# Moving modulation sums and mLSTM's end within the projection stage of a hybrid decoder block

## The chip, the cores and the metric

The kernel runs on one core of a Trainium2 chip. A core has five engines that run side by side and meet only at semaphores: PE (TensorE, matrix products and transposes), DVE (VectorE), ACT (ScalarE), POOL (GpSimd) and SP (SyncE, which here issues every DMA). Each engine works through its own instructions strictly in order, so an instruction that waits holds up all that stand behind it on the same engine. The metric is the device time of one execution in microseconds (us); lower is better. Numbers of lines (L1045) are those of the kernel before unless it is said otherwise.

## The reference, cut to what matters

One decoder layer with 2048 positions of width 1024, in float32:

```python
mod = silu(c) @ w_ada + b_ada          # six vectors of 1024: shift, scale, gate, twice
sh1, sc1, gt1, sh2, sc2, gt2 = split(mod, 6)
h = rms_norm(x, g_mix) * (1 + sc1) + sh1
p = h @ w_in                            # q,k,v (512 each), q_m,k_m,v_m,o_m (256), u_s,v_s (256), gates
y_attn = forgetting_attention(rms_norm(q_a), rms_norm(k_a), v_a, f_a)      # 8 heads of 64
hm = mlstm_chunkwise(q_m, k_m, v_m, i_m, f_m)                              # 4 heads of 64
hm = rms_norm(hm, g_m_out)                                                 # over each head's 64
y_mlstm = sigmoid(o_m) * hm
y_sgu = spatial_gating(gelu(u_s), gelu(v_s), g_sgu, w_s, b_s)
x = x + gt1 * (concat(y_attn, y_mlstm, y_sgu) @ w_out)
h = rms_norm(x, g_ffn) * (1 + sc2) + sh2
x = x + gt2 * conv_ffn(h, w_up, w_conv, b_conv, w_down)
```

The first shift and scale are needed ahead of everything. The other four vectors (two gates, second shift and scale: 4096 columns) are needed only after the mixer, and the kernel works them out in small portions beside the projections.

## The kernel before, in words

The kernel runs through the projections (about 60 to 720 us), the attention, the output product and the channel MLP. Only the projections concern the change.

*Blocks and steps.* The 2048 positions are taken in two halves of 1024; for each half the columns of `w_in` are taken in seven blocks, in this order: k_m with the gates, q_m with o_m, v_m, the spatial unit (u and v), k, q, v. That makes 14 blocks, counted from 0: the spatial unit is block 3 (first half) and 10 (second half), k is 4 and 11, q is 5 and 12, v is 6 and 13. A block has eight row tiles of 128 positions. A float32 product is made of three products of rounded parts (`mm3`, L53 to L56), so a tile is 8 x 3 = 24 matmuls on PE. After the tile's 12th matmul, in blocks 512 columns wide, and after its last, `products` calls `tick`: 16 steps in a wide block, 8 in a narrow one. Behind a tile's last step the block's own work on that tile is issued (`consume`): for q and k the squares L768 on ACT, their sums L770 on DVE, the inverse root on POOL (L128, called `rsqrt`); one step later the scaling `qn` L776 on DVE; three steps after that the four transposes L784 on PE, then L788 on ACT and L789 on DVE. For the spatial unit: a layer norm per tile (L705 to L722, with POOL's L712 and L128 in it), and after every fourth tile four mixes (PE's L735, DVE's L736 and L737; groups 0 and 1 in one step, 2 and 3 in the next) and two turns (L744). PE's results for these pass through a few shared banks, so a matmul into a bank waits until the last result in it has been read.

*A step* (`tick`) does three things. First it issues what `after(n, f)` has put off until this step. Then, at middle steps alone (those after the 12th matmul), it takes one step of `chores`, which holds the modulation sums. Then it takes one step of the first generator in `background`: `rows` and `mlstm`, first come, first served, each advancing to its next `yield`. Blocks 1 to 5 and 8 to 12 keep the order as it is written here; blocks 0, 6, 7 and 13 are put in order by the framework's scheduler.

*Modulation sums* (`rest_of_mod`, from L452). There are eight column groups of 512, each the sum over eight row tiles of `w_ada`: 64 sums. A sum is one DVE instruction of 128x512 (L466 for the first of a group, L468 for the others); it issues the load of the next 256 KB tile of `w_ada` on SP (L458). The seventh also loads the bias row; with the eighth, DVE adds that row (L474), and two steps later `columns_or_row` makes either four narrow matmuls (L488, for shift and scale) or one 512-wide one (L482, for the gates, with ACT's L484 and a store behind it).

*mLSTM* (`mlstm(qi)`, qi = 0 to 3, 512 positions each) works through four chunks of 128 positions and then has an end. `mlstm(0)` and `mlstm(2)` enter the queue in block 2 and 9, and run beside the spatial unit; `mlstm(1)` and `mlstm(3)` follow them and run beside k and q. The end is: DVE makes the denominator (L1029 to L1032) and divides (L1034, 128x1024); SP loads the gate `om` (L1036); ACT squares (L1038, into `hq`); DVE sums the squares (L1040) and scales (L1041); POOL raises to the power -1/2 (L1042, 128x16). Two steps later DVE multiplies, `hq = hn * ss` (L1045, 128x1024). Two steps later PE makes eight transposes of `hq` (L1052), and DVE multiplies by the norm's weight and by `om` (L1054) and SP stores.

*Beside these*, `products` splits the next block's weights into two parts: ACT's cast L595 and DVE's difference L596, and loads them (L585). In front of the first half's v block, SP also loads the first four row tiles of `x` for the second half (L404), which ACT squares (L518) and DVE scales (L523).

*At block 13* a loop ran what was left in `background` to its end before the score matmuls of the attention's first heads (L206) entered it.

Of the kernel before, what the change touches and what calls it, by code (L numbers as in the profile page):

```python
# [12 lines left out]
ALU = mybir.AluOpType  # L13
# [20 lines left out]
def trunk(  # L34
# [7 lines left out]
    V, A, G, T = nc.vector, nc.scalar, nc.gpsimd, nc.tensor  # L42
# [4 lines left out]
    def bc(ap, axis, n):  # L47
        u = ap.unsqueeze(axis)
        shape = list(u.shape)
        shape[axis] = n  # L50
        return u.broadcast_to(shape)
# [86 lines left out]
    def attention_open_right():  # L138
        pool.open("att_s", "right", ("nm", 8, 6), ("rs", 8, 6))
        pool.open("att_r", "right", ("kvA", 8192, 3), ("LA", 4096, 8), ("qA", 2048, 6))  # L140
        pp.open("att_r", "right", ("sp", 4096, 2))
# [19 lines left out]
    def load_v(h, cs):  # L161
        for c in cs:
            dma(
                kv[h][2][:, 4 * c : 4 * c + 4].bitcast(F32),
                v_d[c * TB : (c + 1) * TB, h, :].rearrange("(n p) d -> p n d", p=P),
            )
# [208 lines left out]
    def misc_ps():  # L375
        return pp.tile([P, 512], F32, name="mp", tag="mp")
# [25 lines left out]
    def load_x(tt):  # L402
        xt = pool.tile([P, D], F32, name="xt", tag="t4k")
        dma(xt, x[tt * P : (tt + 1) * P, :])  # L404
        return xt
# [43 lines left out]
    def rest_of_mod():  # L449

        seq = [(col, k) for col in (3072, 3584, 4096, 4608, 2048, 2560, 5120, 5632) for k in range(KT)]
        tiles = {}  # L452

        def load(i):
            if i < len(seq):
                col, k = seq[i]
                tiles[i] = pool.tile([P, 512], F32, name="wa", tag="t2k")
                dma(tiles[i], w_ada[k * P : k * P + P, col : col + 512])  # L458

        load(0)  # L460
        yield
        for i, (col, k) in enumerate(seq):
            st = tiles.pop(i)
            if k == 0:
                acc = pool.tile([P, 512], F32, name="modacc", tag="macc")
                V.tensor_scalar(acc, st, cs[:, 0:1], None, op0=ALU.mult)  # L466
            else:
                V.scalar_tensor_tensor(acc, st, cs[:, k : k + 1], acc, op0=ALU.mult, op1=ALU.add)  # L468
            load(i + 1)
            if k == 6:  # L470
                brow = pool.tile([1, 512], F32, name="brow", tag="t2k")
                dma(brow, b_ada[:, col : col + 512])
            if k == 7:
                V.tensor_tensor(acc[0:1, :], acc[0:1, :], brow, op=ALU.add)  # L474
                after(2, lambda acc=acc, col=col: columns_or_row(acc, col))
            yield

    def columns_or_row(acc, col):
        kind, half = col // 1024, (col % 1024) // 512
        ps = misc_ps()  # L480
        if kind in (2, 5):
            T.matmul(ps, ones, acc, start=True, stop=True)  # L482
            gr = pool.tile([1, 512], F32, name="gr", tag="t2k")
            A.copy(gr, ps[0:1, :])  # L484
            dma(gt_d[kind // 3 : kind // 3 + 1, half * 512 : half * 512 + 512], gr)
        else:
            for j in range(4):
                T.matmul(ps[:, j : j + 1], acc[:, j * P : (j + 1) * P], ones[:, 0:1], start=True, stop=True)  # L488
            sl = slice(half * 4, half * 4 + 4)
            if kind == 3:  # L490
                V.tensor_copy(sh2[:, sl], ps[:, 0:4])
            else:
                V.scalar_tensor_tensor(
                    a2[:, sl], ps[:, 0:4], 1.0, gf[:, half * 4 : half * 4 + 4], op0=ALU.add, op1=ALU.mult
                )
# [126 lines left out]
    pending = []  # L622
    chores, started = [], []
    background = []
    ticks = [0]

    def tick(middle=False):
        ticks[0] += 1
        due()
        if middle and chores and started and next(chores[0], True):  # L630
            chores.pop(0)
        if background and next(background[0], True):
            background.pop(0)
# [15 lines left out]
    def after(n, f):  # L649

        pending.append((ticks[0] + n, f))

    def due(everything=False):
        for item in pending[:]:
            if everything or item[0] <= ticks[0]:
                pending.remove(item)
                item[1]()
# [267 lines left out]
    def mlstm(qi):  # L925
# [52 lines left out]
        for n in range(4):  # L978
# [44 lines left out]
            if n < 3:  # L1023
                decay(n + 1)
                yield

        den = pool.tile([P, 4, 4], F32, name="den", tag="den")
        nd = pool.tile([P, 4, 4], F32, name="nd", tag="nd")
        V.tensor_scalar(nd, H[:, :, :, 64], -1.0, None, op0=ALU.mult)  # L1029
# [3 lines left out]
        hn = H[:, :, :, 0:64]  # L1033
# [2 lines left out]
        dma(om, om_d[:, :, t0 : t0 + 512].rearrange("j p t -> p j t"))  # L1036
        hq = pool.tile([P, 4, 4, 64], F32, name="hq", tag="t4k")
        A.activation(hq, hn, AF.Square)  # L1038
        ss = pool.tile([P, 4, 4], F32, name="mss", tag="mss")
        V.tensor_reduce(ss, hq, axis=AX.X, op=ALU.add)  # L1040
        V.tensor_scalar(ss, ss, 1.0 / 64, EPS, op0=ALU.mult, op1=ALU.add)  # L1041
        G.tensor_tensor(ss, ss, nhalf[:, 0:1].unsqueeze(2).broadcast_to([P, 4, 4]), op=ALU.pow)  # L1042
        yield
        yield
        V.tensor_tensor(hq, hn, bc(ss, 3, 64), op=ALU.mult)  # L1045
        hq2 = hq.rearrange("p n h d -> p n (h d)")
        yield
        yield
# [18 lines left out]
    nb = len(blocks)  # L1067
    steps = [(h, i) for h in range(2) for i in range(nb)]
    chores.append(rest_of_mod())
    written = ExitStack()  # L1070
    cur = Weights(blocks[0][0], G, ("q2k",) * 3 + ("qhl",) * 3 + ("wr",) * 2)
# [5 lines left out]
    for n, (half, i) in enumerate(steps):  # L1077
        if i == 0:
            make_h(half * 2, x0)
            if half == 0:  # L1080
                head_setup()
            make_h(half * 2 + 1)
        elif n == nb - 1:
            x0 = [load_x(8 + t) for t in range(4)]
        if n == len(steps) - 1:
            while background:
                if next(background[0], True):
                    background.pop(0)
            n_accs[0] = 2
            pool.close("proj_r")  # L1090
            pp.close("proj_r")
            attention_open_right()

            load_k(0)
            first_rows = [], []
            first = [scores(0, tb, load_q(0, tb, "qA"), r) for tb, r in zip((1, 0), first_rows)]
            load_v(0, (0, 1))
            background += first
        nxt[0] = Weights(blocks[steps[n + 1][1]][0]) if n + 1 < len(steps) else None
        if i == 1:  # L1100
            written.enter_context(tc.manual_schedule())
        blocks[i][1](half, cur)
        started.append(n)
        if nxt[0]:
            nxt[0].cast()
        cur = nxt[0]
        if n in (nb - 2, 2 * nb - 2):
            written.close()
        if i == 0:
            log_gates(half)  # L1110
            background += [rows(half * 2), rows(half * 2 + 1)]
        if i == 2:
            background.append(mlstm(half * 2 + 1))
        if n == nb + 2:
            small_setup()
# [630 lines left out]
```

## Time and profile before

| | us |
|---|---|
| three runs | 2606.87, 2607.7, 2610.26 |
| median | 2607.7 |
| the profiled execution | 2607.8 |
| its span | 2606.1 |
| PE idle in the span | 75.6 (2606.1 - 2530.5) |

The profiled execution's mean granted clock of PE is 0.997 of full speed. 1.7 us lie around the span. The page names an instruction by its engine and line, and an operand by the program's name. A "wait" is idle time of an engine ahead of an instruction, put down to the instruction elsewhere that released it. Matmuls overlap, so the durations of neighbouring ones add up to more than their distance in time: a matmul of 128x512 shows 0.39 us and the next begins 0.23 us later.

### The profile page before, as it was taken

How to read it: one execution, taken by the hardware profiler on the slowest of the kernel's cores; microseconds unless marked ns; L12 is line 12 of the kernel's file. 1: busy time of each engine (PE TensorE's matmuls, PEld its weight loads, DVE VectorE, ACT ScalarE, POOL GpSimd, SP SyncE). 2: the span in 40 equal slices, each digit the busy share in tenths (PEclk: the TensorE clock that was granted, in tenths of full speed). 3: DMA queues.
4: the chain of work that ended last, by engine and by line, in shares of the span. 5: the costliest groups of instructions: out<-in, count | busy, mean ns of one | idle time of the engine just before them, and what ended most of it. 6: DMA issues, size and time to landing. Idle time of an engine off the chain costs nothing.

```text
span 2606.1 us, 36311 instructions
## 1 busy us (share of the span) xinstructions
PE 2530.5 (97%) x12521; PEld 2097.9 (81%) x12537; DVE 2010.0 (77%) x3438; ACT 1272.8 (49%) x2424; POOL 402.5 (15%) x532
## 2 busy tenths in 40 slices
PE   5999999999999999999989999999999999999999
PEld 5888888888787877777868888888888888888787
DVE  7657666476388889866589888888888887997797
ACT  4333343432388878844455544454444444444443
POOL 2012310132266556520000000000000000000000
PEclk9999999999999999999999999999999999999999
DMA  7345763454664445266632222255222217658523
GB/s 247 107 120 160 209 209 88 129 152 138 180 164 123 129 126 166 58 195 224 248 89 92 79 89 82 81 201 187 90 81 81 90 65 279 210 176 290 184 93 117
DMA packets 302592, 379.58 MB, mean 146 GB/s; under 512 B 31934, under 2 KB 194588, under 8 KB 300360
## 3 DMA queue, kind: packets, MB, share of 16 engines
q1 hardware_dynamic: 302408, 377.26, 46.1%
q8 instruction: 99, 1.62, 0.3%
q14 instruction: 85, 0.70, 0.1%
HBM read 276.44 MB, written 100.74 MB: 145 GB/s over the span
## 4 chain that ended last, share of the span: by engine, by line
PE 81%; DVE 9%; DMA 4%; ACT 3%; issue 2%; POOL 1%; SPq 0%; DVEq 0%; ACTq 0%; POOLq 0%
PE ub L56 11%; PE ub L54 11%; PE ub L55 11%; PE acc L54 6%; PE acc L56 6%; PE acc L55 6%; PE db L55 4%; PE db L56 4%; PE db L54 4%; PE sp L206 3%; PE tp L259 3%; PE op L245 2%; PE op L246 2%; PE wps L55 2%; PE wps L54 2%
## 5 line engine op out<-in xcount | busy, mean ns | idle before, releaser
L54 PE MATMUL acc<-wh,hh 128*128 128x512 f32 (+2 forms) x768 | 285.5, 373 | 1.9 <-DVE vhl L762 1.2
L54 PE MATMUL ub<-T,wsph 128*128 128x512 f32 x704 | 274.2, 390 | 5.8 <-ACT wsph L1358 5.8
L56 PE MATMUL ub<-T,wspl 128*128 128x512 f32 x704 | 273.7, 389 | 1.6 <-DVE wspl L1359 1.6
L56 PE MATMUL acc<-wh,hl 128*128 128x512 f32 (+2 forms) x768 | 274.2, 360 | 0.3 <-DVE hl L566 0.3
L55 PE MATMUL acc<-wl,hh 128*128 128x512 f32 (+2 forms) x768 | 273.9, 358 | 0.2
L55 PE MATMUL ub<-T,wsph 128*128 128x512 f32 x704 | 273.9, 389 | 0.0
L55 PE MATMUL db<-wspl,wsph 128*128 128x512 f32 x616 | 240.6, 391 | 3.6 <-DVE wspl L1490 3.5
L56 PE MATMUL db<-wsph,wspl 128*128 128x512 f32 x616 | 239.6, 389 | 0.0
L54 PE MATMUL db<-wsph 128*128 128x512 f32 x616 | 238.3, 389 | 0.3 <-ACT wsph L1489 0.3
L1358 ACT CAST wsph<-S 128x512 fp32r<-128x512 f32 x176 | 109.7, 623 | 228.4 <-PE ub L55 162.8
L263 DVE TENSOR_TENSOR plo<-tp,phi 128x512 fp32r<-128x512 f32 (+1 forms) x320 | 187.0, 607 | 31.6 <-ACT phi L262 29.4
L54 PE MATMUL ub<-B,wsph 128*128 128x512 f32 x528 | 207.1, 392 | 2.8 <-ACT wsph L1358 2.8
L56 PE MATMUL ub<-B,wspl 128*128 128x512 f32 x528 | 207.2, 392 | 0.6 <-DVE wspl L1359 0.6
L55 PE MATMUL ub<-B,wsph 128*128 128x512 f32 x528 | 207.0, 392 | 0.0
L223 ACT ACTIVATE L<-L,nm 128x1024 f32<-128x1024 f32 (+2 forms) x192 | 172.6, 903 | 36.0 <-DVE nm L212 34.7
L262 ACT CAST phi<-tp 128x512 fp32r<-128x512 f32 (+1 forms) x320 | 160.0, 521 | 40.2 <-PE tp L259 38.9
L259 PE MATMUL tp<-ident,L 128*128 128x128 f32 x1088 | 177.0, 274 | 2.5 <-POOL L L228 0.6
L206 PE MATMUL sp<-kk,q 128*128 128x512 f32 (+3 forms) x640 | 169.2, 375 | 3.3 <-DVE nm L212 2.2
L1489 ACT CAST wsph<-act 128x512 fp32r<-128x512 f32 x132 | 82.3, 623 | 179.0 <-PE db L55 162.2
L228 POOL TENSOR_SCALAR L<-L,rs 128x1024 f32<-128x1024 f32 (+2 forms) x192 | 167.2, 881 | 11.0
L56 PEld LDWEIGHTS acc<-wh,hl 128*128 128x128 f32 x768 | 145.0, 190 | 22.3 <-DVE hl L566 0.8
L54 PEld LDWEIGHTS acc<-wh,hh 128*128 128x128 f32 x768 | 146.2, 191 | 20.7 <-DVE vhl L762 1.4
(333 smaller groups left out, 5942.9 us busy)
## 6 DMA issues: line engine op xcount, KB each, us to landing
w<-in_w_up_dram SPq DMA_DIRECT2D x88, 512.0 KB
wd<-in_w_down_dram SPq DMA_DIRECT2D x176, 256.0 KB
wa<-in_w_ada_dram SPq DMA_DIRECT2D x96, 256.0 KB
act_d<-yc SPq DMA_DIRECT2D x44, 512.0 KB
act<-act_d SPq DMA_DIRECT2D x44, 512.0 KB
wr<-in_w_in_dram SPq DMA_DIRECT2D x64, 256.0 KB
q<-q_d SPq DMA_DIRECT2D x128, 128.0 KB
hc_d<-hl SPq DMA_DIRECT2D x28, 512.0 KB
```

The costliest lines, as they stand in the source:

```text
L54: T.matmul(ps, lh, rh, start=start, stop=False, skip_group_check=resume)
L55: T.matmul(ps, lh, rl, start=False, stop=False, skip_group_check=resume)
L56: T.matmul(ps, ll, rh, start=False, stop=stop, skip_group_check=resume)
L206: T.matmul(sp[:, b : b + bw], q2[n][:, qs], kk[:, s0 + b : s0 + b + bw], start=n == 0, stop=n == 1 and not last)
L223: A.activation(L[c], L[c], AF.Exp, bias=nm[:, n - 1 : n], scale=-1.0, accum_out=rs[:, c : c + 1])
L228: G.tensor_scalar(t, t, rs[:, 0:1], 1.0, op0=ALU.mult, op1=ALU.mult)
L245: T.matmul(op[:, c0:], vv[:, j, :], hi[:, c0:], start=(j == 0), stop=False)
L259: T.transpose(tp[:, i * P : (i + 1) * P], rows[i][j // 8][:, (j % 8) * P : (j % 8 + 1) * P], ident)
L262: A.copy(hi[:, c0:], tp[:, c0:])
L263: V.tensor_tensor(lo[:, c0:], tp[:, c0:], hi[:, c0:].bitcast(F32), op=ALU.subtract)
L1358: A.copy(hi, src)
L1489: A.copy(hi, v)
```

## The change

Four edits, all in the order of work; what is computed is the same.

1. `tick` counts the steps of the running block. The modulation sums are taken in all 16 steps of block 5; at the middle steps of blocks 1, 4, 6, 8, 11 and 12 and in step 2 of block 12; and in none of blocks 3 and 10 (before: the middle steps of every wide block from block 1 on until the sums were done).
2. The column products follow the bias sum by one step, not two.
3. The end of `mlstm(0)` and `mlstm(2)` begins four steps later, so it moves from the spatial unit's last steps to the k block's first; since `mlstm(1)` and `mlstm(3)` queue behind them, these start later too, and their ends lie in the q block's steps 8 to 14 (before: 2 to 6). In every end one more step lies between the Square and its sum, and one more between the power and the product; the product L1045 is issued on POOL (L1053 of the changed kernel).
4. At block 13, the loop that empties `background` becomes an assertion that nothing is left, and that the sums are finished.

```diff
             if k == 7:
                 V.tensor_tensor(acc[0:1, :], acc[0:1, :], brow, op=ALU.add)
-                after(2, lambda acc=acc, col=col: columns_or_row(acc, col))
+                after(1, lambda acc=acc, col=col: columns_or_row(acc, col))
...
-    ticks = [0]
+    ticks, in_block = [0], [0, 0]
 
     def tick(middle=False):
         ticks[0] += 1
         due()
-        if middle and chores and started and next(chores[0], True):
+        block = started[-1] + 1 if started else 0
+        in_block[0] = in_block[0] + 1 if in_block[1] == block else 1
+        in_block[1] = block
+        if chores and (block == 5 or (block, in_block[0]) == (12, 2) or middle and block in (1, 4, 6, 8, 11, 12)) and next(chores[0], True):
             chores.pop(0)
...
+        if qi % 2 == 0:
+            for _ in range(4):
+                yield
         den = pool.tile([P, 4, 4], F32, name="den", tag="den")
...
         A.activation(hq, hn, AF.Square)
+        yield
         ss = pool.tile([P, 4, 4], F32, name="mss", tag="mss")
...
         G.tensor_tensor(ss, ss, nhalf[:, 0:1].unsqueeze(2).broadcast_to([P, 4, 4]), op=ALU.pow)
         yield
         yield
-        V.tensor_tensor(hq, hn, bc(ss, 3, 64), op=ALU.mult)
+        yield
+        G.tensor_tensor(hq, hn, bc(ss, 3, 64), op=ALU.mult)
...
         if n == len(steps) - 1:
-            while background:
-                if next(background[0], True):
-                    background.pop(0)
             n_accs[0] = 2
...
+            assert not background and next(chores.pop(), True)
             background += first
```

## The prediction

> **What bounds the kernel now.** I read the page's first part first, then its chain that ended last: TensorE is busy for 97% of the span, and four fifths of the chain is its matmuls. A change of vector work can only pay where PE itself stands.
>
> ```profile
> PE 2530.5 (97%) x12521; PEld 2097.9 (81%) x12537; DVE 2010.0 (77%) x3438; ACT 1272.8 (49%) x2424; POOL 402.5 (15%) x532
> PE 81%; DVE 9%; DMA 4%; ACT 3%; issue 2%; POOL 1%; SPq 0%; DVEq 0%; ACTq 0%; POOLq 0%
> ```
>
> The edits lie between 60 and 720 us. The view of waits, for PE alone in that stretch, gives what PE waited for there (total, times, longest, in us), all of it:
>
> ```profile
> PE mps L1052 <- DVE hq L1045: 6.8, 4, 2.7
> PE trp L560 <- ACT h L564: 2.1, 1, 2.1
> PE acc L54 <- DVE vhl L762: 1.2, 1, 1.2
> PE sp L206 <- DVE nm L212: 1.0, 3, 0.7
> PE trp L560 <- DVE xt L523: 1.0, 3, 0.5
> ```
>
> The first line is the wait of mLSTM's transposes for its last product, once per 512 positions. The view by windows places it (columns: stretch, length, then busy time of PE, PEld, DVE, ACT, POOL, the granted clock, DMA share, GB/s):
>
> ```profile
> 200.00:220.00 20.00, 17.31 (x84) 14.11 (x83) 17.28 (x37) 7.04 (x14) 9.97 (x7) 1.00 0.32 105
> 280.00:300.00 20.00, 19.12 (x99) 15.86 (x98) 12.47 (x27) 4.58 (x7) 6.13 (x3) 1.00 0.66 193
> 300.00:320.00 20.00, 20.00 (x96) 16.53 (x95) 12.60 (x23) 5.05 (x9) 6.55 (x4) 1.00 0.90 276
> 540.00:560.00 20.00, 17.31 (x81) 13.84 (x80) 15.55 (x36) 4.77 (x10) 9.50 (x7) 1.00 0.54 166
> 620.00:640.00 20.00, 19.50 (x99) 16.13 (x98) 10.61 (x19) 4.09 (x8) 9.29 (x5) 1.00 0.50 144
> ```
>
> Each 17.31 is one 2.69 us stand in a spatial unit's last steps (for positions 0 to 511 and 1024 to 1535); 19.12 and 19.50 are the stands beside the q block. Elsewhere PE is full (20.00), so any wait that arises anew there is paid in whole.
>
> The timeline at the first stand (start, us, engine, line, ...; idle before and its releaser in brackets) shows the chain:
>
> ```profile
> 203.89 1.22 DVE L1034 TENSOR_TENSOR H<-H,den 128x1024 f32<-128x1024 f32 x1
> 205.20 1.06 ACT L1038 ACTIVATE hq<-H 128x1024 f32<-128x1024 f32 x1 [10.40 <-DVE H L1034]
> 206.29 1.22 DVE L1040 TENSOR_REDUCE mss<-hq 128x16 f32<-128x1024 f32 x1 [1.19 <-ACT hq L1038]
> 207.80 3.27 POOL L1042 TENSOR_TENSOR mss<-mss,nhalf 128x16 f32<-128x16 f32 x1 [3.88 <-DVE mss L1041]
> 211.04 0.91 POOL L712 TENSOR_TENSOR ev<-ev 128x256 f32<-128x256 f32 x1
> 213.17 1.22 DVE L1045 TENSOR_TENSOR hq<-H,mss 128x1024 f32<-128x1024 f32 x1
> 214.53 1.06 PE L1052 MATMUL mps<-ident,hq 128*128 128x128 f32 x8 [2.69 <-DVE hq L1045]
> ```
>
> The power was done at 211.07, but the product went at 213.17: it stood on DVE behind the spatial unit's variance, which waited for POOL's L712, and behind a modulation sum.
>
> **The change, part by part** (line numbers of the kernel before).
>
> *The gain: 6.8 us, firmly.* The product goes to POOL, one more step lies before it, and two steps more between product and transposes remain. No row shows a 128x1024 product of two tiles on POOL. Its nearest row is the 128x256 product, L995, and the lower end is a 128x1024 product by one number per row, L228:
>
> ```profile
> L995 POOL TENSOR_TENSOR kw<-kn,ecol 128x256 f32<-128x256 f32 x16 | 9.8, 611 | 162.0 <-DMA kn<-km_d 162.0
> L228 POOL TENSOR_SCALAR L<-L,rs 128x1024 f32<-128x1024 f32 (+2 forms) x192 | 167.2, 881 | 11.0
> L468 DVE SCALAR_TENSOR_TENSOR modacc<-wa,cs,modacc 128x512 f32<-128x512 f32 x56 | 41.8, 746 | 7.4 <-DMA wa<-in_w_ada_dram 7.1
> L474 DVE TENSOR_TENSOR modacc<-modacc,brow 1x512 f32<-1x512 f32 x8 | 5.4, 679 | 0.2
> ```
>
> Four times 0.611 is 2.4 us, with 0.9 (L228) and 3.6 (four times the disturbed L712 of 0.91) as ends; I take 2.4, as L995 is the same operation. Two steps between emission and transposes are a row tile, 5.9 us (below), so the product is there in time in all four places, even where POOL starts it 2 us late. All four waits go: -6.8.
>
> *The q block's new wait: +4.9 us, once.* All 16 steps of block 5 now hold a sum (before: 8), so a column of eight sums ends at the block's 9th step, the step after mLSTM's end for positions 512-1023 begins; and its column product L488 stands one step after the bias sum L474 instead of two. So L488 enters PE's queue directly behind the next tile's transposes L784. What L474 is queued behind on DVE I time from the same stretch of before:
>
> ```profile
> 281.78 0.60 PE L784 MATMUL trp<-ident,qn 128*128 128x128 f32 x4
> 283.13 0.75 DVE L789 SCALAR_TENSOR_TENSOR qlo<-trp,colA,qhi 128x512 fp32r<-128x512 f32 x1 [0.52 <-ACT qhi L788]
> 283.80 0.17 DVE L1029 TENSOR_SCALAR nd<-H 128x16 f32<-128x16 f32 x1
> 284.71 1.22 DVE L1034 TENSOR_TENSOR H<-H,den 128x1024 f32<-128x1024 f32 x1
> 285.97 1.06 ACT L1038 ACTIVATE hq<-H 128x1024 f32<-128x1024 f32 x1 [2.87 <-DVE H L1034]
> 286.93 0.58 ACT L768 ACTIVATE qsq<-acc 128x512 f32<-128x512 f32 x1
> 288.63 0.60 PE L784 MATMUL trp<-ident,qn 128*128 128x128 f32 x4
> 293.10 0.69 DVE L776 TENSOR_TENSOR qn<-acc,ss 128x512 f32<-128x512 f32 x1 [3.75 <-POOL ss L128]
> 294.55 0.60 PE L784 MATMUL trp<-ident,qn 128*128 128x128 f32 x4
> 295.89 0.68 DVE L770 TENSOR_REDUCE ss<-qsq 128x8 f32<-128x512 f32 x1
> 296.92 1.64 POOL L128 TENSOR_TENSOR ss<-ss,nhalf 128x8 f32<-128x8 f32 x1 [3.86 <-DVE ss L771]
> ```
>
> Take L784 as 0. DVE's qlo starts at 1.35 (283.13 - 281.78); then the 8th step's sum, new there, at 2.0; mLSTM's L1029 at 2.7 (2.02 before, plus about 0.7); the division's end, 2.1 us later (283.80 to 285.93), at 4.8; ACT's Square L1038, 1.06 us and what lies between, to 5.9. The squares qsq of the tile just ended stand behind that Square on ACT, so their sum ss starts on DVE at about 6.5. From ss to qn is 2.7 us (295.89 to the end of POOL's 296.92 + 1.64, 298.56, plus a little): qn at 9.2. In the changed order the 9th step's sum comes behind qn (9.8), then L474 (10.5 to 11.2). PE reaches L488 at 5.92 (288.63 to 294.55, a tile without mLSTM) plus 0.4 of L784, 6.35. Wait: 11.25 - 6.35 = 4.9 us. The ends: 3.5, if the 8th step's sum goes late without holding L1029 and the rows' gaps are shorter; 6, if POOL's power takes 2.0 us instead of 1.64 and the bias row comes late. In the second half no column ends there, so it happens once.
>
> *The spatial unit's mixes: +2.3 us, in two places.* mLSTM's end for the half's first 512 positions now begins at the k block's first step. DVE gets the block's sum with L474 (0.75 + 0.68), then L1029 to L1034 (2.1), and PE's L735 for groups 2 and 3 needs the two transpose banks that DVE's L736 for groups 0 and 1 empties; those stand behind the first tile's qn, which waits for POOL. On POOL mLSTM's power (3.27 us above) now goes ahead of that tile's own. Before:
>
> ```profile
> 223.65 0.69 DVE L776 TENSOR_TENSOR qn<-acc,ss 128x512 f32<-128x512 f32 x1 [1.57 <-POOL ss L128]
> 225.19 0.42 DVE L736 TENSOR_TENSOR sy<-trp,gsgu 128x256 f32<-128x256 f32 x1 [0.45 <-PE trp L735]
> 228.18 1.02 PE L735 MATMUL trp<-sv,wT 128*128 128x256 f32 x4
> ```
>
> L736's first read ended at 225.61, 2.57 us before PE came with groups 2 and 3: that is the slack. With the stand gone PE comes 2.69 us earlier, at 225.49. The new chain: from the sum's start 1.4 (0.75 + 0.68), 2.1, Square 1.1, L1040 and its scaling 1.4, POOL's power 3.3, the tile's own 1.6, and 2.0 from qn to the end of the first L736 (223.65 to 225.61), 12.9 us together. If the sum starts as PE comes to its step, at 211.84 (214.53 - 2.69), the bank is free at 224.7: no wait. If DVE comes to it 3.5 us later, held by the spatial unit's last tile as before (L1045 alone kept it until 214.39), it is free at 228.2: 2.7. I take 1.2 of 0 to 2.7, near the middle: 2.3 for both halves.
>
> *The step into the v block: +2.4 us.* SP now issues three of the four loads of x back to back behind mLSTM's load of om, and in ACT's changed order four of the row squares L518 stand directly ahead of the last weight's cast, which its split on DVE needs:
>
> ```profile
> 329.12 0.64 ACT L518 ACTIVATE jk<-xt 128x512 f32<-128x512 f32 x1
> 330.93 0.67 DVE L596 TENSOR_TENSOR wl<-wr,wh 128x512 fp32r<-128x512 f32 x1
> ```
>
> Four at 0.64 are 2.6 us; about half is covered by what the old order waits for anyway, so some 1.2 us on the v block's first tile, which needs that weight; and the next column's L488, again one step behind its L474, some 1.2 more. Ends: 0 and 4.
>
> *At nothing.* The sums taken from the spatial units (8 of each) free DVE where it is 17.28 of 20 us busy; PE is full behind them but for the stand counted above. The sums in block 12 and the second half's later mLSTM lie where DVE is busy for 10.6 of 20 us; without that cover each sum would cost its 0.75. The drain loop that goes at the last block ran over an empty list. A sum's load is issued by the same step, so it moves too; in the spatial unit SP's queue is shorter by 8 loads, in block 5 longer by 8.
>
> Sum: -6.8 + 4.9 + 2.3 + 2.4 = +2.8 us. The profiled execution took 2607.8 us (a span of 2606.1 and 1.7 around it), 0.1 above the median of the runs shown: 2610.6, or 2610.5 on the median.
>
> **The rivals.**
>
> *Faster: no new wait forms.* DVE is idle for 7.5 of 20 us beside the q block; if the chain there is shorter than I count, or the order of engines gives L488 its step of room, only the gain stays: 2607.7 - 6.8 = 2601. Against it: the qn in the middle of the chain waits for POOL in nearly every tile,
>
> ```profile
> L776 DVE TENSOR_TENSOR qn<-acc,ss 128x512 f32<-128x512 f32 x32 | 22.1, 691 | 50.7 <-POOL ss L128 50.7
> ```
>
> and L474 now stands behind one.
>
> *A wash: only the q block's wait forms.* -6.8 + 4.9: 2606. For it: the spatial term and the v block's are both near the slack.
>
> *Slower: POOL's product holds up DVE.* L712 took 0.91 us beside DVE's split of weights where L995 took 0.61: the two get in each other's way. If a DVE instruction that falls into the product's 2.4 us stands until it is over, then in the q blocks qn and the sums behind it are late: qn ended at 293.79, 0.76 us before L784 at 294.55, so from 0.8 us on PE pays. That is 2.4 - 0.8 = 1.6 us at each of four products, about 6 with what DVE then lacks for sums: 2616. Against it: the row shows 0.3 us lost, by POOL, and not by DVE. [...]
>
> *Slower: late modulation weights.* The 56 sums of the L468 row waited 7.1 us for their loads. Issued at twice the rate beside block 5, the loads could come late again by as much in all, where DVE has no room to catch up (past 0.8 us a tile): 2610.5 + 7, 2617.
>
> **The numbers.** Forecast 0.45, only the q block's wait 0.15, no new wait 0.1, DVE held by POOL 0.2, late weights 0.1. A measurement of this kernel tells about 0.2%, 5.2 us, from no change: faster is below 2602.5, slower above 2612.9. Faster: the case without waits and a little of the wash, 0.12. Slower: the last two, and a part of the forecast whose terms run to their upper ends (6, 5.2 and 4 give +8.4): 0.34. The rest, 0.54, is the same. The low end takes in most of the case without waits, 2602; the high end the held DVE, 2616.
>
> **What would show it.** In the changed profile: no wait of L1052 for hq on PE (if one is left, the gain is wrong); PE's L488 beside the first half's q block waiting for DVE's L474 for 4 to 5 us (if below 1, the faster cases hold); the third and fourth L735 behind L736, twice; a gap before the v block's first tile. [...] The forecast is wrong if PE's idle time between 60 and 720 us falls by more than 4 us or grows by more than 9.

## The result, and the profile after

The changed kernel takes 2621.74 us (median of 5 runs, 2621.31 to 2624.18), the kernel before 2606.87 (5 runs, 2604.58 to 2610.26): a ratio of 1.0059, 95% interval 1.0046 to 1.0073. The forecast was 2610.5 in a range up to 2616. The profiled execution of the changed kernel has a span of 2619.7 us, 13.6 more than that of before. (Line numbers of the changed kernel lie a little behind those of before: L1052 is L1060 there, L1045 is L1053, L784 is L787, L735 is L738; L468 to L488 are the same.)

From the page of the changed kernel, its line of engines and the chain that ended last:

```profile
PE 2537.6 (97%) x12537; PEld 2101.7 (80%) x12537; DVE 2009.9 (77%) x3434; ACT 1272.9 (49%) x2424; POOL 405.8 (15%) x536
...
PE 77%; DVE 10%; DMA 5%; ACT 3%; issue 3%; POOL 2%; SPq 1%; DVEq 0%; ACTq 0%; POOLq 0%
```

PE is busy 7.1 us longer, though the work is the same: most of that, as the rows below show, is work at a lower clock. The mean granted clock was 0.992 to 0.994 in all five executions; the kernel before, in its executions beside the experiments, had 0.994 to 0.998. The chain went less through PE and more through DVE, DMA and POOL. PE's waits between 60 and 720 us (total, times, longest, in us):

```profile
PE mp L488 <- DVE modacc L474: 6.8, 2, 4.7
PE mp L482 <- DVE modacc L474: 5.2, 1, 5.2
...
PE mps L1006 <- DVE sc L992: 1.5, 2, 0.8
...
PE trp L738 <- DVE sy L739: 1.0, 4, 0.4
...
PE acc L55 <- DVE wl L596: 0.4, 1, 0.4
```

The 6.8 us in front of mLSTM's transposes are gone altogether. In their place stand 12.0 us in front of column products: 4.7 beside the first half's q block, 2.05 on the way into the v block, 5.2 at the end of block 12. The stretches of 20 us (stretch, length, then busy time of PE, PEld, DVE, ACT, POOL, granted clock, DMA share, GB/s) show a second loss behind each of them:

```profile
200.00:220.00 20.00, 20.00 (x98) 16.66 (x97) 13.41 (x31) 7.10 (x14) 9.11 (x7) 1.00 0.49 157
300.00:320.00 20.00, 15.27 (x66) 12.61 (x65) 12.65 (x25) 5.32 (x9) 8.37 (x4) 0.83 0.73 231
340.00:360.00 20.00, 17.95 (x79) 14.59 (x78) 12.89 (x29) 3.87 (x10) 1.53 (x3) 0.91 0.69 204
660.00:680.00 20.00, 14.80 (x56) 11.02 (x55) 13.26 (x23) 4.72 (x9) 4.63 (x3) 0.83 0.78 213
```

PE is full now in the spatial unit's last steps (20.00 in place of 17.31), with DVE at 13.41 in place of 17.28. But the clock, 1.00 everywhere in this stage before, falls to 0.83, 0.91 and 0.83 just where the three column products wait. In stretches of 2 us at the first of them:

```profile
304.00:306.00 2.00, 0.00 (x0) 0.00 (x0) 0.57 (x2) 1.77 (x4) 1.25 (x1) 1.00 0.91 255
306.00:308.00 2.00, 0.00 (x0) 0.00 (x0) 1.54 (x3) 0.00 (x0) 0.39 (x1) 0.60 1.01 396
308.00:310.00 2.00, 1.46 (x7) 1.46 (x8) 1.97 (x4) 0.00 (x0) 0.10 (x1) 0.50 0.92 377
310.00:312.00 2.00, 2.00 (x6) 1.71 (x7) 2.00 (x5) 0.00 (x0) 2.00 (x1) 0.50 0.25 64
312.00:314.00 2.00, 2.00 (x7) 1.56 (x7) 0.31 (x2) 0.00 (x0) 2.00 (x2) 0.69 1.03 325
```

PE is back at 308.54 (next fence) and then works at half clock to about 313.2: its 128x512 matmuls begin 0.43 us apart there, and 0.23 behind it. By the granted clock that is 1.46 x 0.5 + 2 x 0.5 + 2 x 0.31 = 2.35 us lost. Worked out the same way, 1.7 us are lost at the second place and 2.7 at the third, 6.75 in all.

The chain at the first place, from the timeline of DVE, ACT, POOL and PE:

```profile
300.88 1.23 DVE L1040 TENSOR_TENSOR H<-H,den 128x1024 f32<-128x1024 f32 x1
302.14 1.06 ACT L1044 ACTIVATE hq<-H 128x1024 f32<-128x1024 f32 x1 [3.54 <-DVE H L1040]
303.11 0.57 ACT L771 ACTIVATE qsq<-acc 128x512 f32<-128x512 f32 x1
303.21 0.60 PE L787 MATMUL trp<-ident,qn 128*128 128x128 f32 x4
303.72 0.69 DVE L773 TENSOR_REDUCE ss<-qsq 128x8 f32<-128x512 f32 x1 [1.61 <-ACT qsq L771]
304.75 1.64 POOL L128 TENSOR_TENSOR ss<-ss,nhalf 128x8 f32<-128x8 f32 x1 [9.87 <-DVE ss L774]
306.42 0.69 DVE L779 TENSOR_TENSOR qn<-acc,ss 128x512 f32<-128x512 f32 x1 [1.81 <-POOL ss L128]
307.81 0.68 DVE L474 TENSOR_TENSOR modacc<-modacc,brow 1x512 f32<-1x512 f32 x1
308.54 1.87 PE L488 MATMUL mp<-ones,modacc 128*128 128x1 f32 x8 [4.73 <-DVE modacc L474]
```

This is link by link the chain that the prediction timed. At the end of block 12 it is longer, and the new product on POOL takes part in it:

```profile
646.78 0.69 DVE L779 TENSOR_TENSOR qn<-acc,ss 128x512 f32<-128x512 f32 x1 [1.81 <-POOL ss L128]
...
649.54 3.27 POOL L1049 TENSOR_TENSOR mss<-mss,nhalf 128x16 f32<-128x16 f32 x1 [2.80 <-DVE mss L1048]
...
654.39 1.90 POOL L1053 TENSOR_TENSOR hq<-H,mss 128x1024 f32<-128x1024 f32 x1
654.45 0.69 DVE L779 TENSOR_TENSOR qn<-acc,ss 128x512 f32<-128x512 f32 x1 [2.93 <-POOL ss L128]
655.06 1.77 DVE L468 SCALAR_TENSOR_TENSOR modacc<-wa,cs,modacc 128x512 f32<-128x512 f32 x1
...
660.64 0.69 DVE L779 TENSOR_TENSOR qn<-acc,ss 128x512 f32<-128x512 f32 x1 [1.75 <-POOL ss L128]
...
663.17 1.40 DVE L1062 SCALAR_TENSOR_TENSOR yt<-mps,colA,om 128x512 f32<-128x512 f32 x2
667.50 0.69 DVE L779 TENSOR_TENSOR qn<-acc,ss 128x512 f32<-128x512 f32 x1 [0.32 <-POOL ss L128]
668.88 0.68 DVE L474 TENSOR_TENSOR modacc<-modacc,brow 1x512 f32<-1x512 f32 x1
669.61 2.07 PE L482 MATMUL mp<-modacc,ones 128*128 128x512 f32 x2 [5.20 <-DVE modacc L474]
```

mLSTM's power held up a tile's own root on POOL (qn waited 2.93 us), a sum beside the product took 1.77 us and not 0.74, and mLSTM's last products L1062 stood ahead of the next tile's sum. So DVE's scalings qn came 7.67, 6.19 and 6.86 us apart, while PE's transposes L787 came 5.92, 5.93 and 6.80 us apart (644.23, 650.15, 656.08 and 662.88). Seven steps after mLSTM's end began DVE was still late when the last column came due.

How it adds up in the projection stage: -6.8 (transposes) + 12.0 (column products) + 1.0 (L738) + 1.5 (L1006) + 0.4 (wl) + 6.75 (low clock) = +14.9, against 13.6 more in the span. From the first L735 or L738 to the first score matmul L206 the rows give 479.2 us before (193.9 to 673.1) and 497.9 after (191.7 to 689.6), 18.7 more. 1.8 of that is an order changed at block 13 (eight acc matmuls more ahead of the first L206, at 0.23 us), given back behind it; about 1 more is a column product (eight L488) that now stands behind the first mix and stood ahead of it before; some 1 us I can't place. The rest of the span is 5.1 us shorter, so that the sum of 14.9 lies near the 13.6 is partly luck.

### The profile page after: what moved, and what is told of

It is laid out like the page before. It is cut to its first block, busy times and chain, and to the rows that moved or that the text cites. A ratio compares the mean times of both kernels' runs of the same rounds, so it can differ in the third digit from the quotient of the medians.

```text
span 2619.7 us, 36342 instructions
## 1 busy us (share of the span) xinstructions
PE 2537.6 (97%) x12537; PEld 2101.7 (80%) x12537; DVE 2009.9 (77%) x3434; ACT 1272.9 (49%) x2424; POOL 405.8 (15%) x536
## 4 chain that ended last, share of the span: by engine, by line
PE 77%; DVE 10%; DMA 5%; ACT 3%; issue 3%; POOL 2%; SPq 1%; DVEq 0%; ACTq 0%; POOLq 0%
PE ub L56 11%; PE ub L54 10%; PE ub L55 10%; PE acc L54 5%; PE acc L56 5%; PE acc L55 5%; PE db L55 4%; PE db L56 4%; PE db L54 4%; PE sp L206 3%; PE tp L259 3%; PE op L245 2%; PE op L246 2%; DVE wspl L1496 2%; PE wps L56 2%
## 5 line engine op out<-in xcount | busy, mean ns | idle before, releaser
L206 PE MATMUL sp<-kk,q 128*128 128x512 f32 (+3 forms) x640 | 169.9, 377 | 3.8 <-DVE nm L212 2.7
```

The source lines that it names most:

```text
L206: T.matmul(sp[:, b : b + bw], q2[n][:, qs], kk[:, s0 + b : s0 + b + bw], start=n == 0, stop=n == 1 and not last)
```

## The experiments

Each kernel ran beside the kernel before on the same chip; ratios are to that. A stand is PE's idle time ahead of a matmul that waits; the three columns give PE's stands ahead of column products, of matmuls that wait for the split weights (wl and wh), and of mLSTM's transposes, in us. They are from one profile of each kernel, and the low clock is not in them. The profiled executions of e4, e5, e10 and e14 took 2616.1, 2615.3, 2616.0 and 2644.7 us, 2.3 to 6.5 above the medians of their kernels, so their stands need not be those of a median execution.

| kernel | column products | wl and wh | mLSTM's transposes | ratio, 95% interval |
|---|---|---|---|---|
| changed | 12.0 | 0.4 | 0 | 1.0059 (1.0046 to 1.0073) |
| e1: two steps, but for the last column | 8.5 | 1.0 | 0 | 1.0042 (1.0027 to 1.0057) |
| e7: two steps everywhere | 5.8 | 0.6 | 0 | 1.0035 (1.0022 to 1.0048) |
| e9: three steps | 2.0 | 4.2 | 0 | 1.0012 (1.0003 to 1.0021) |
| e8: filler matmuls | 3.1 | 1.7 | 0 | 1.0047 (1.0032 to 1.0062) |
| e3: product on DVE | 10.6 | 0.8 | 1.6 | 1.0063 (1.0049 to 1.0077) |
| e4: before + mLSTM's edits | 0 | 6.5 | 0 | 1.0016 (1.0006 to 1.0026) |
| e6: before + sums moved | 1.0 | 2.2 | 6.5 | 1.0017 (1.0008 to 1.0026) |
| e2: before + one step | 1.1 | 0 | 7.0 | 1.0012 (1.0001 to 1.0022) |
| e5: before + product on POOL | 0 | 0.5 | 8.4 | 1.0016 (1.0007 to 1.0025) |
| e10: before, transposes a step later | 0 | 7.6 | 0 | 1.0006 (0.9997 to 1.0015) |
| e11: changed without the four steps | 16.1 | 4.4 | 0 | 1.0104 (1.009 to 1.0118) |
| e12: e11 with two steps | 5.9 | 4.2 | 0.4 | 1.0031 (1.0019 to 1.0042) |
| e13: 8 sums in block 5, 16 in 8 | 5.9 | 8.8 | 0 | 1.0091 (1.0074 to 1.0108) |
| e14: no sums in 3, 5, 10, 12 | 0.8 | 18.7 | 0 | 1.0119 (1.0104 to 1.0134) |
| e15: sums in early steps | 0 | 6.4 | 0.4 | 1.0041 (1.0029 to 1.0054) |
| e16: e10 with sums out of the spatial unit | 1.5 | 2.7 | 0 | 0.9991 (0.9982 to 1.0) |
| e17: e16 with three steps | 0.2 | 4.5 | 0 | 0.9982 (0.9973 to 0.9991) |

**How much is the one step?** e1 and e7 put the column product back to two steps (in e7 a further sum in block 12, in step 4, keeps the last column inside the block).

```diff
-                after(1, lambda acc=acc, col=col: columns_or_row(acc, col))
+                after(2, lambda acc=acc, col=col: columns_or_row(acc, col))
```

> The changed kernel, but the column products follow the bias sum by two steps again, except the last column's, which keeps one step. Theory A (the loss is PE standing in front of column products, and running at half clock for some microseconds behind each such stand): the stands beside the q block (4.7 us) and at the v block (2.05) go, with the time at half clock behind them (2.35 and 1.6), the one at the end of block 12 stays (5.2 and 2.7): 2621.7 - 10.7 = 2611. Rival B (block 5 is overfull: 16 sums with their loads make DVE late, and PE waits wherever DVE is late): the waits move to other instructions of the same blocks, and the time stays above 2618. Rival C (POOL's product holds up DVE): above 2618 too.

> The changed kernel with two steps between bias sum and column product everywhere, and one more sum in step 4 of block 12, so that the last column still ends inside that block. Theory A: no stand before a column product, no half clock, and the gain of 6.8 us at mLSTM's transposes stays, less about 2.5 us of small new waits (L738 and L1006): 2603 to 2605, faster than before by 3 to 5 us. Rival B or C: above 2612.

Both misses. I had taken the step for the cause, and it buys 12 matmuls and no more; e7's waits of PE:

```profile
PE mp L488 <- DVE modacc L474: 3.3, 2, 2.0
PE mp L482 <- DVE modacc L474: 2.5, 1, 2.5
```

4.73 became 1.97 and 5.20 became 2.46, each 2.75 shorter. In e7 the last column ends two steps earlier in block 12 and L474 was just as late behind its step. e9 allows three steps, and sums in steps 2, 4 and 6 of block 12:

> The changed kernel with three steps between bias sum and column product, and sums also in steps 4 and 6 of block 12. A step is 12 matmuls, 2.75 us; the kernel with two steps showed each stand shorter by just that (4.73 to 1.97, 5.20 to 2.46), so with three steps 1.97 - 2.75 is below zero. Theory A2 (the bias sum is late by a fixed time, set by what is queued ahead of it on DVE, and the step count only decides how much of it PE sees): no stand before a column product, no low clock from one, the gain of 6.8 us less about 2.5 us of small waits is left: 3 to 5 us below the kernel before. If DVE's lateness shows up at other instructions instead (weights' split, transposes of q): no gain, 2 to 6 us above it.

```profile
PE acc L55 <- DVE wl L596: 3.3, 2, 3.1
...
PE mp L488 <- DVE modacc L474: 1.1, 1, 1.1
...
PE mp L482 <- DVE modacc L474: 0.9, 1, 0.9
```

The column products are nearly quiet, and DVE's lateness comes out at the split of the v block's weights instead, the second of the two outcomes that were named.

**Is the low clock a cost of its own?** e8 lets PE work through the two long stands.

```diff
         ps = misc_ps()
+        if started and started[-1] + 1 in (5, 12) and col in (4096, 5632):
+            for r in range(20):
+                fh, fl = hT[2 * (started[-1] > 6), r % KT]
+                T.matmul(ps, fh[:, 0:P], fh, start=True, stop=True)
```

> The changed kernel with 20 matmuls without use (128x512, into the bank that the column product then overwrites) ahead of the column product beside the q block and of the last one in block 12: PE works through both stands. The results are those of the changed kernel. If the half clock behind a stand is a cost of its own that comes from PE's idleness, it goes in both places while L474 ends as late as before: 2.35 + 2.7 = 5.0 us less than the changed kernel, 2616.7, with a granted clock of 1.00 behind both. If the low clock has another cause, or the fillers cost what they save: 2621 or more.

The same stretch as above, beside the q block, in e8:

```profile
306.00:308.00 2.00, 2.00 (x11) 1.62 (x10) 0.18 (x2) 1.27 (x3) 1.64 (x1) 1.00 0.92 302
308.00:310.00 2.00, 1.88 (x9) 1.22 (x7) 1.97 (x4) 0.00 (x0) 0.00 (x0) 1.00 1.03 418
```

The clock stays at 1.00 there and at block 12's end, while L474 still comes late (1.6 us of stand are left at block 12's end, where the fillers ran out). From the first mix of the spatial unit to the first score matmul e8 took 493.7 us (193.3 to 687.0) where the changed kernel took 497.9: 4.2 of the expected 5.0. Two places without fillers differ as well and about cancel: on the way into the v block the clock stayed at 1.00 behind a stand of 1.35 us (1.7 us less lost), and at 383 us it fell for 3.4 us where the changed kernel's did not (1.7 us more). The whole time doesn't show the gain clear of the noise, 1.0047 against 1.0059, with intervals that overlap. What the profile shows is that at these two places the low clock (0.50 in the changed kernel) goes when PE is kept at work, though the data come as late: there it follows PE's idleness, and is a cost beside the wait.

**Each part by itself.** e4 has mLSTM's edits alone, e6 the new places of the sums alone (with two steps, and a sum in step 4 of block 12), e2 the one step alone, e5 the product on POOL alone.

> The kernel before with the edits of mLSTM's end alone (four steps later for the first 512 positions of a half, one more step at two places, the product on POOL); sums and column products as before. Theory A: the four waits at L1052 go (-6.8), about 2.5 us of small waits come, no stand above 2 us arises: 2602 to 2605. Rival C (POOL's product is what costs): slower than before, 2610 or more, with DVE instructions stretched beside the product.

> The kernel before with the sums placed as in the changed kernel (none beside the spatial unit, all 16 steps of block 5; in block 12 also step 4) and two steps before the column product; mLSTM's end as before. Theory A2 (the column's end is late because mLSTM's end now falls just ahead of it): mLSTM's end is at step 2 here, the column's end at step 9, so L474 is on time and no column product waits over 0.5 us; L1052 still waits, less in the spatial unit where a sum of 0.74 us no longer stands ahead of L1045: 5 to 6 us in all; the time is the same as before within 2 us. Rival B (block 5 overfull with sums): L488 waits over 2 us all the same, 2612 or more.

> The kernel before with one step between bias sum and column product, nothing else. There L474 ends 4.7, 1.5, 3.8 and 4.5 us before its L488 comes in the first half's blocks 3 to 6; a step is 2.75 us, so only block 4 (and 11 like it) should wait, 1.2 us each: 2 to 3 us slower than before, up to 6 if the clock falls behind one.

> The kernel before with the product on POOL, nothing else. POOL is free at 211.95 in the spatial unit (behind L712), so the product of 1.90 us ends at 213.85, not 214.39 on DVE: the stands there shrink by 0.5 us, those beside the q block (0.88, 0.5) go, as POOL's product ends about 1 us earlier there. A sum beside it is held up by 1 us. 6.8 us of wait become 4.3: 2 us faster than before, within 2. Rival C (POOL's product makes DVE late, and that costs): 3 us slower or more.

e2 came out as expected in time, with one stand of 1.1 us instead of two. The others missed: e4 and e5 were to gain and e6 to break even, and each lost some 0.16%. For e4 that is a mean of two groups: six executions took 2607.3 to 2609.9 us at a mean clock of 0.996 or 0.997, four took 2613.5 to 2617.7 at 0.993 or 0.994, and the profile is of one of the four. In e4 the four waits went, as they should, but with 8 sums in block 5, none of which ends a column behind mLSTM's end, the v block's split of weights waited:

```profile
PE acc L54 <- ACT wh L595: 3.9, 2, 3.1
PE acc L55 <- DVE wl L596: 2.6, 4, 1.1
```

In e5 the product had to stand on POOL behind the spatial unit's own root, which I had left out of its queue:

```profile
212.49 1.44 POOL L128 TENSOR_TENSOR mu<-mu,nhalf 128x4 f32<-128x4 f32 x1 [0.74 <-DVE mu L717]
213.91 1.90 POOL L1045 TENSOR_TENSOR hq<-H,mss 128x1024 f32<-128x1024 f32 x1
```

It ended at 215.8, not 213.85, and the stand there grew from 2.7 to 4.2 us. The other way round, e3 takes only POOL's product back out of the changed kernel:

> The changed kernel with the product back on DVE, nothing else. Beside POOL's product the DVE sum L468 took 1.77 us (three times) and 1.26 us, not 0.74. Theory A2: the stands before column products stay (4.7, 2.0 and about 5: the product on DVE takes 1.22 us there, about what the hold-up took), the sums beside it take 0.74 us again: within 3 us of the changed kernel. Rival C (POOL's product is what makes DVE late): the stand at block 12's end falls below 3 us and the time by 4 us or more.

The stand at block 12's end went from 5.2 to 3.9, the other two stayed, 1.6 us came back at the transposes: the product on POOL makes 1.3 us of lateness at one place and pays for itself elsewhere. The whole time is the same within the noise (1.0063 against 1.0059), so the product on POOL is not the cause.

**The four steps, or the sums?** e11 takes the four steps (`if qi % 2 == 0: for _ in range(4): yield`) out of the changed kernel, e12 has two steps to the column product besides, and a sum in step 4 of block 12.

> The changed kernel without its four steps of delay for mLSTM's first 512 positions of a half; sums, the one step, the further steps and POOL's product as changed. mLSTM's end for the other positions is then four steps earlier in the q block, at steps 4 to 10, and its Square no longer falls just ahead of the column's end at step 9. Theory A3 (the four steps are what makes the bias sum late): the stand of 4.7 us beside the q block goes to below 1, that at block 12's end (5.2) to below 2, with the low clock behind them: 2621.7 - 4.7 - 2.3 - 4 - 2.7 = 2608, within 3. Rival B (16 sums in block 5 alone make it late): the stands stay over 3 us, 2615 or more.

> As the kernel without the four steps, and with two steps before the column product (and a sum in step 4 of block 12). Theory A3: what waits are left before column products go, 2602 to 2606. Rival B: the lateness goes to the weights' split in front of the v block (over 2 us), 2608 or more.

e11 refuted the theory plainly: 1.0104. The stand beside the q block grew to 6.4 us, with mLSTM's end four steps further ahead of the column's. e12 came out as its rival B had it: 4.2 us of waits at the split, 1.0031. The rows of e11 beside the q block show why the distance didn't help (mLSTM's power is L1046 there):

```profile
298.29 0.60 PE L787 MATMUL trp<-ident,qn 128*128 128x128 f32 x4
...
301.51 0.69 DVE L779 TENSOR_TENSOR qn<-acc,ss 128x512 f32<-128x512 f32 x1 [1.81 <-POOL ss L128]
...
304.22 0.60 PE L787 MATMUL trp<-ident,qn 128*128 128x128 f32 x4
304.28 2.90 POOL L1046 TENSOR_TENSOR mss<-mss,nhalf 128x16 f32<-128x16 f32 x1 [2.80 <-DVE mss L1045]
...
308.81 0.69 DVE L779 TENSOR_TENSOR qn<-acc,ss 128x512 f32<-128x512 f32 x1 [2.49 <-POOL ss L128]
309.42 1.77 DVE L468 SCALAR_TENSOR_TENSOR modacc<-wa,cs,modacc 128x512 f32<-128x512 f32 x1
...
315.06 0.69 DVE L779 TENSOR_TENSOR qn<-acc,ss 128x512 f32<-128x512 f32 x1 [1.75 <-POOL ss L128]
```

PE takes 5.93 us for a tile (298.29 to 304.22). DVE took 7.30 and 6.25 us from one qn to the next: in the first tile mLSTM's power stood on POOL ahead of the tile's own root, in the second its product held the sum L468 for 1.77 us. So the later parts of mLSTM's end had come to lie in the tiles just ahead of the column's end. Without them DVE can catch up, but slowly. In e6, where mLSTM's end is over by then, a tile with two sums took 5.39 us, only 0.54 less than PE's:

```profile
303.40 0.69 DVE L779 TENSOR_TENSOR qn<-acc,ss 128x512 f32<-128x512 f32 x1 [1.81 <-POOL ss L128]
...
308.79 0.69 DVE L779 TENSOR_TENSOR qn<-acc,ss 128x512 f32<-128x512 f32 x1 [1.81 <-POOL ss L128]
```

DVE looks far from full there (busy for 12 to 13 of 20 us in both), but in nearly every tile it stands 1.75 us or more for POOL's root.

Three doses of sums in block 5, with mLSTM's end late as in the changed kernel: 16 (changed), 8 (e13, the others in block 8) and none (e14, the others in every step of 1, 2, 8 and 9).

> The changed kernel with all 16 steps of a sum in block 8 instead of block 5; block 5 has 8, at its middle steps, and no column ends there behind mLSTM's end. If the number of sums in block 5 makes DVE late (theory B2): no wait of L488 there, and the waits for DVE from block 5's end to the v block's first tile fall from 2.45 us (2.05 + 0.4) to below 1; block 12 has not changed, so its stand of 5.2 stays: 2621.7 - 4.7 - 2.3 - 2.05 - 1.6 = 2611. If mLSTM's late end alone is enough (theory A4, for which the kernel before with the late end speaks, which had 8 sums there and 6.5 us of waits for the split of weights): L488's wait is replaced by 3 us or more of waits for wh and wl, 2614 or more.

> The changed kernel with no sums in blocks 3, 5, 10 and 12 (all steps of 1, 2, 8 and 9, the middle steps of 4 and 6, one in 11). Theory B2 (sums beside mLSTM's end are what makes DVE late): no column product waits over 0.5 us, no split over 1 us, the four waits at L1052 stay gone; 2.5 us of small waits stay: 3 to 5 us faster than the kernel before. Theory A4 (mLSTM's late end makes DVE late without any sum): waits for wh and wl of 3 us or more at the v block and at block 13: the same as before or slower.

Both were far slower. The wait moved to the split of weights: on the way into the v block (320 to 365 us) it was 4.2 us in e13 and 2.7 in e14, which has no sum in block 5 at all. More came up where a block had a sum in every step. e14's waits of PE between 60 and 720 us, then of DVE:

```profile
PE acc L55 <- DVE wl L596: 13.9, 8, 3.2
PE acc L54 <- ACT wh L595: 4.8, 4, 2.5
```

```profile
DVE modacc L468 <- DMA wa<-in_w_ada_dram: 54.0, 23, 7.1
```

The sums waited 54 us for their loads, issued only a step ahead (before: 7.1). So the whole times of e13 and e14 do not isolate block 5's sums; they show what a sum in every step costs. e15 keeps mLSTM's late end with no sum behind it in the q block, but with one in each of the seven steps ahead of it:

> The changed kernel with its mLSTM edits, two steps before the column product, and the 64 sums so placed that none stands beside an end of mLSTM in the q block: in blocks 5 and 12 in steps 1 to 7 alone, in 1 and 8 in steps 1 to 8 and the later middle steps, 11 in block 6, middle steps in 4 and 11. Theory A5 (a sum queued between mLSTM's end and the block's last steps makes DVE late, DVE's lateness holds back the splits that free the buffers for weights, and SP's one queue then holds every other load): the stand at block 12's end and beside the q block goes, waits at the v block's entry below 1.5 us, low clock only by chance: 3 us below the kernel before. Theory A4 (mLSTM's late end alone is enough): 3 us or more of waits for wl and wh at the entries to blocks 6 and 13: as before or up to 5 us slower.

It has 6.4 us of waits for wl and wh, all on the way into the v block. With e4 and e14's 2.7 us this speaks for theory A4: the late end alone makes DVE late there. How much the sums ahead of it add in e15 is not shown.

**A version faster than both.** e10 only puts one more step between product and transposes in the kernel before; e16 besides takes the sums out of the spatial unit and into early steps of other blocks; e17 gives the column products of the second shift and scale three steps.

```diff
         yield
         yield
+        yield
         for j in range(2):
             yp = mps()
```

> The kernel before with one more step between the product L1045 (still on DVE) and its transposes, nothing else. The product ended at 214.39 and PE stood from 211.84; a step is 2.75 us, so the transposes come at 214.6, after it: the four waits of 6.8 us go. mLSTM's other half ends one step later, at the q block's steps 3 to 8, far from the split of the next block's weights. Theory A3 (an early end of mLSTM in the q block costs nothing, a late one hands DVE's lateness to whatever comes next): no new stand above 1 us, 5 to 7 us faster than before: 2601. If the moved end of positions 512-1023 collides as in the changed kernel: 2606 or more.

> The kernel before, its mLSTM with the product on DVE and one more step between product and transposes, and no sums beside the spatial unit (middle steps of 4, 5, 11 and 12, steps 1 to 8 and later middle steps of 1 and 8, 10 in block 6). With sums beside the spatial unit the one step turned 6.8 us of waits at L1052 into 7.6 us of waits for wl. Theory A5: without them DVE is a sum of 0.74 us earlier at each block's end there, the waits for wl at the k block's entry fall from 1.6 to about 0.9 each, those at L1052 stay gone: 2 to 5 us below the kernel before. If the waits for wl stay at 7 us in all: as before.

> The kernel before with one more step ahead of mLSTM's transposes and the sums in early steps, none beside the spatial unit, as the last but one run; with three steps, not two, before the column products of the second shift and scale. There L488 stood 1.3 us once, and the clock was low for 3.4 us behind it. If PE's stands and the low clock behind them are the whole difference, 1.3 + 1.7 = 3 us come off: 2603 to 2604 on a kernel before of 2607.5, a ratio near 0.998. If the wait moves to the split of weights: no gain, ratio 0.999 to 1.000.

e10 is a lesson by itself: 6.8 us of waits for hq became 7.6 for wl, for the stand at the transposes had hidden DVE's lateness at the split behind it. With the sums out of the spatial unit (e16) those 7.6 became 2.7, and e17 is the only kernel clearly faster than before: 2602.2 us, ratio 0.9982 (0.9973 to 0.9991). In its profile the transposes and L488 wait no more; the split still does, for 4.5 us. That e17 is faster than e16 is not shown: the intervals meet, and the 1.3 us that went at L488 came back as 1.8 more at the split.

## Why the prediction was wrong, point by point

- *The gain of 6.8 us at the transposes: right.* All four waits are gone. The product took 1.90 us on POOL (2.4 forecast, bounds 0.9 and 3.6).
- *The q block's new wait, +4.9: right in place, chain and size.* 4.73 measured. With 297.28 as 0 (a tile ahead of L787 at 303.21), qn came at 9.14 (9.2 forecast) and L474 ended at 11.21 (11.25).
- *The spatial unit's mixes, +2.3: too dear.* 1.0 at L738; but 1.5 arose at L1006, which had no term.
- *The step into the v block, +2.4: right in the sum, by luck.* It was forecast as 1.2 for the last weight's split and 1.2 for L488; 0.4 and 2.05 were measured.
- *"In the second half no column ends there, so it happens once": the step that failed first.* The last column ends at block 12's 15th step and its product stands one step behind, seven steps after mLSTM's end began. I took it for granted that DVE had caught up by then and entered block 12 at nothing. It cost 5.2 us. e7 shows the bias sum just as late two steps earlier in the block, and the changed kernel's rows show why it stays late: in the three tiles behind 646.78 DVE took 20.7 us where PE took 18.65. What little it gains in a tile without mLSTM's end (0.54 us with two sums, in e6) could not make that good in time. The average that I leaned on (DVE busy for 10.6 of 20 us) counts its waits for POOL as free time.
- *The price of a stand: the step that failed second.* Every stand entered the sum with its own length. Behind each of the three, PE also worked at half clock, at a loss of 6.75 us in all, for which the sum had no term. e8 shows it apart from the wait, in one profile.
- *The sum.* +2.8 forecast; 5.2 + 6.75 + 1.5 more and 1.3 less at the mixes give +14.9, and the medians differ by as much (2621.74 - 2606.87 = 14.9). That they agree so closely is luck: the stage alone grew by 18.7 us.
- *The rivals.* "DVE held by POOL" has its row (1.77 us in three places, 1.26 in the fourth) but not its price: e3 finds 1.3 us at one place. That a DVE instruction which falls into the product stands until it is over was a supposition, and the rows bear it out in part: at all four products the sum L468 ended about 0.5 us after the product, while qn beside it took its usual 0.69 us. "Late modulation weights" is small here (DVE's waits for them went from 7.1 to 10.8 us) and large in e14. Neither was the cause; the range's upper end, which they set at 2616, was too low because both unpriced costs came together.

## What to carry to other kernels

An engine that waits for another in every tile has less slack than its busy share says: take its period from one repeated instruction to the next, and compare that with the tile of the bounding engine before putting work on it (5.39 against 5.93 us here, with DVE busy for 12 of 20). A removed wait is worth only what the next late thing behind it leaves (e10); look for who is late next, and move the cause rather than the place where it shows. In this kernel a stand of PE of 2 us or more is to be priced with a chance of 1.7 us or more of lost clock behind it; the last section counts how often.

## What the runs showed of the hardware

*The clock after a stand.* Low stretches, at a granted clock of 0.50 in the changed kernel, began while PE stood or shortly behind it, and one and the same stand brought them in one execution and not in another. In the 19 profiles, between 60 and 720 us, a low stretch began in the stand or within 3.4 us behind it at all 9 stands of 3.8 us or more, at 24 of 32 between 2.0 and 3.2 us, and at 22 of 61 between 1.2 and 2.0 us. The second half's spatial unit makes PE stand 2.69 us in the kernel before, with a clock of 1.00 (its 540 to 560 row, in the prediction). In e2 the stand was 2.70 us there, and the clock fell:

```profile
540.00:560.00 20.00, 17.30 (x75) 13.85 (x73) 14.96 (x34) 6.29 (x14) 9.56 (x6) 0.91 0.48 147
```

In the changed kernel the low stretches were 6.83 us long at the stands of 4.73 and 5.20 us and 3.41 us at the one of 2.05. Below 3.8 us the length of a stand alone does not tell whether one comes: in e16 1.32 us was enough, while 3.07 us in e9 brought none. Why the clock falls, no run shows. Part of the spread between executions of one kernel goes with the clock, as e4's two groups show (0.996 or 0.997 against 0.993 or 0.994).

*A sum beside POOL's product.* In all four places of the changed kernel the sum L468 that began while the product of 1.90 us ran ended about 0.5 us after the product did, in block 12 at 656.83 against 656.29. It took 1.77 us in three of them and 1.26 in the fourth; the other 52 took 0.74 to 0.75. qn, which began less than 0.1 us behind the product in each place, took its usual 0.69. What sets the two apart, no run shows.
